# A Mixer's output stage in another order of queues, and the adaLN products moved back by three steps

## The chip, the core and the metric

The kernel runs on one NeuronCore of one Trainium2 chip. The core has five engines, each with its own instruction queue that runs strictly in order: TensorE (PE in the profile; its weight loads are PEld), VectorE (DVE), ScalarE (ACT), GpSimd (POOL) and SyncE (SP), which here only issues DMAs. PE writes its results into PSUM, eight banks of 128 x 512 f32, and the others read them there. The metric is the device time of one execution in microseconds, given as the median of several runs; lower is better.

## The reference

One layer of a streaming encoder on 1024 tokens of width 1024, f32. Three residual sub-layers, each conditioned on a vector `c`:

```python
def sandwich(x, fn, g_pre, g_post, shift, scale, gate, res_w):
    h = modulate(rmsnorm(x, g_pre), shift, scale)
    y = rmsnorm(fn(h), g_post)
    return x + res_w * gate[:, None, :] * y

mod = (silu(c) @ w_ada + b_ada).reshape(b, 3, 3, D_MODEL)        # shift, scale, gate of each sub-layer
x = sandwich(x, swiglu_1, ..., mod[:, 0, 0], mod[:, 0, 1], mod[:, 0, 2], 0.5)
x = sandwich(x, mixer,    ..., mod[:, 1, 0], mod[:, 1, 1], mod[:, 1, 2], 1.0)
x = sandwich(x, swiglu_2, ..., mod[:, 2, 0], mod[:, 2, 1], mod[:, 2, 2], 0.5)

def mixer(h, ...):                       # q k v xr yr g_att g_rec = split(h @ w_in)
    att = chunked_attention(q, k, v, rel_bias) @ w_att_o
    rec = (rg_lru(conv(xr)) * gelu(yr)) @ w_rec_o
    return (sigmoid(g_att) * att + sigmoid(g_rec) * rec) @ w_out
```

The change concerns two places: the product with `w_out` with the residual and the norm behind it, up to the first matmuls of `swiglu_2`; and the part of `mod` that belongs to the Mixer's gate and to the second SwiGLU, which is computed beside the product with `w_rec_o`.

## The kernel before

Every f32 operand of a matmul is split into a high part (rounded to the matmul's f32r format, by a copy on ACT) and a low part (the difference, by a subtraction on DVE); a product is then three matmuls, high x high, high x low, low x high (`split`, L147; `mm3`, L488). Matmuls are 128 x 128 by 128 x 512.

**Order of work.** A planner places instructions on the engines by the order of the program text and its own times. Inside `manual_schedule` the order of the text itself is the order on the engines named: in `out_phase` and in the SwiGLUs on PE, DVE, ACT and POOL. The planner always orders SP, and in `rec_out_phase` it orders all engines. A buffer belongs to a tag with a fixed count: a new tile waits until an old one of its tag has been read for the last time. Tag `u` of the scratch pool has three buffers, `raw` (weights as loaded) three, `junk` two. PSUM tag `ps` has six banks, `tr` two. Two engines that touch the same PSUM bank are put one behind the other.

**`rec_out_phase` (L1250).** For each of eight blocks n: the gate product of block n + 1 (48 matmuls), four steps of a background queue, the product with `w_rec_o` of block n (48 matmuls), the merge on DVE and its store, then four more steps of the background queue, each with a step of `out_weights`. After block 7 attention begins (first matmuls L1327).

**The background queue** holds generators (`bg`, L324; one step runs one to its next `yield`). Here they are two column sets, `ada_cols(6)` and `ada_cols(7)`, and two gates, `ada_gate(1)` and `ada_gate(2)`. Each first sums eight blocks of `w_ada`, scaled by `c` (`ada_acc`, L194): a load of 512 KB into `raw` and a DVE operation (L206, L208) per step, into `acc` of tag `u`. `ada_cols` (L214) then makes eight one-column products on PE (L222) and adds the bias on DVE. `ada_gate` (L294) takes two halves: split `acc` (tag `junk`), two matmuls with a matrix of ones (L310, L311) that spread the row over all partitions, add the bias row `bb` (tag `u`, loaded) at L312; at last the scale and a store.

**`out_phase` (L1654).** The 1024 tokens are eight row blocks `sb`, the 1024 columns two halves H1 and H2. The product is by Strassen-Winograd, seven block products (numbers 1, 2, 6, 5, 3, 7, 4), each 48 matmuls, that go into four PSUM banks `chain` (two of tag `ps`, two of tag `tr`) or four private ones. Row blocks 0 to 3 are finished after product 3, the second half of columns of blocks 4 to 7 after product 7, their first half after product 4, which is run for one row block at a time (12 matmuls each). A finished row block goes through these steps:

- `square` (L1676, ACT) of each half with its sum; `gated` (L1683, DVE) multiplies by the gate; `rate` (L1687) makes the reciprocal root, on POOL (L1690);
- `update` (L1693): `epi.update` (L414) adds to the residual row block on DVE (L418) and stores it; `epi.square` (L423) squares the new row block for the next norm on ACT (L342), the root on POOL (L343, L344);
- `epi.norm` (L429) scales the row block by that root, on DVE (L435).

When four row blocks have their norm, `epi.drain` (L439) turns the blocks of columns k = 0 to 7 into the next sub-layer's transposed input: four transposes on PE (L379) into one bank, the high part by an activation on ACT (L361), the value in f32 on ACT (L368) or DVE (L370), the low part on DVE (L354). `on_act` says which engine makes the f32 value for even and odd k.

**`head` (L759)** of the second SwiGLU: for its first two blocks of features, eight steps k of six matmuls each on the first 512 tokens (`part`, L596), with a yield behind each step at which `out_phase` puts its own last work; then the same on the other 512 tokens. Step k needs column block k.

Of the kernel before, what the change touches and what calls it, by code (L numbers as in the profile page):

```python
# [27 lines left out]
SB = S // P  # L28
# [7 lines left out]
HEAD_WAIT = 13  # L36
# [2 lines left out]
SHARE = (3, 4, 4, 5, 5)  # L39
LEFT = 40.0  # L40
GATES = (2, 0, 2, 4)
NORM_ACT = ()
DIRECT = {0: 4, 2: 3}
KEPT_FROM = 5

# [4 lines left out]
def kernel(  # L50
# [160 lines left out]
        yield None  # L211
        yield acc

    def ada_cols(v):  # L214
        acc = None
        for acc in ada_acc(v, tu):
            if acc is None:
                yield
        yield BANK
        pc = trbank("pc")  # L220
        for k in range(KB):
            nc.tensor.matmul(  # L222
                pc[:, k : k + 1], acc[:, k * P : (k + 1) * P], ones[:, 0:1], start=True, stop=True
            )
        sub, kind = divmod(v, 3)
        badd = colsA[:, 8 + v * 8 : 16 + v * 8]
        if kind == 0:
            nc.vector.tensor_tensor(scol[sub], pc[:, 0:KB], badd, op=ALU.add)
        else:
            sc = small("adat", KB)  # L230
            nc.vector.tensor_tensor(sc, pc[:, 0:KB], badd, op=ALU.add)
            nc.vector.scalar_tensor_tensor(
                acol[sub], sc, 1.0, colsA[:, 80 + sub * 8 : 88 + sub * 8], op0=ALU.add, op1=ALU.mult
            )
        yield
# [55 lines left out]
        gtile[sub] = tmp[0].tile([P, D], F32, tag="gate", bufs=1, name=nm("gate"))  # L291
        nc.sync.dma_start(gtile[sub], gate_d[sub])

    def ada_gate(sub, res_w, alloc=tu):  # L294
        v = sub * 3 + 2
        acc = None
        for acc in ada_acc(v, alloc):
            if acc is None:
                yield
        g = tmp[0].tile([P, D], F32, tag="gate", bufs=1, name=nm("gate"))  # L300
        gtile[sub] = g
        bb = tu("bb")
        nc.sync.dma_start(bb, brow(b_ada[0, v * D : (v + 1) * D]))
        for h in range(2):
            sl = slice(h * 512, (h + 1) * 512)
            ah, al = (tmp[0].tile([P, 512], F32R, tag="junk", bufs=2, name=nm("acch")) for _ in range(2))
            split(acc[:, sl], ah, al)
            yield BANK
            pg = trbank("pg")
            nc.tensor.matmul(pg, ones_r, ah, start=True, stop=False)  # L310
            nc.tensor.matmul(pg, ones_r, al, start=False, stop=True)  # L311
            nc.vector.tensor_tensor(g[:, sl], pg, bb[:, sl], op=ALU.add)  # L312
        bb2 = tu("bb2")
        nc.sync.dma_start(bb2, brow(norm_post[0, sub]))
        nc.vector.scalar_tensor_tensor(g, g, res_w, bb2, op0=ALU.mult, op1=ALU.mult)
        if sub in gate_d:
            nc.sync.dma_start(gate_d[sub], g)
        yield
# [63 lines left out]
    class Epilogue:  # L382
# [43 lines left out]
                self.todo.remove(sb)  # L426
                self.r2[sb] = rstd_of(self.xr[sb], EPS)

        def norm(self, sb):  # L429
            if sb not in self.r2:  # L430
                return
            if sb in NORM_ACT:
                nc.scalar.activation(self.y[sb], self.xr[sb], AF.Copy, scale=self.r2.pop(sb))
            else:
                nc.vector.tensor_scalar(self.y[sb], self.xr[sb], self.r2.pop(sb), None, op0=ALU.mult)  # L435
# [1218 lines left out]
    def out_phase(ops, xin, xout, make, start_h, ahead):  # L1654
# [56 lines left out]
        with tc.manual_schedule(engines=CORE_ENGINES):  # L1711
# [42 lines left out]
                rate(i)  # L1754
            for sb in range(3):
                update(sb)
            for j in product(7, chain, False):
                epi.fetch(half + j, t4)
            for i in range(half):
                add(half + i, H2, chain[i])  # L1760
                square(half + i, H2)
                if i == 0:
                    update(3)
                else:
                    epi.norm(i - 1)
            gated(4, H2)
            epi.norm(3)
            start_h()
            for n in range(half):
                sb = half + n  # L1770
                for _ in range(OUT_PAIRS):
                    if n == 0:
                        ops.load(len(ops.order))
                    mm(chain[n], n, 4, _, False, _ == OUT_PAIRS - 1)
                square(sb, H1, chain[n])
                gated(sb, H1, chain[n])
                rate(sb)
                if n < 3:
                    gated(sb + 1, H2)
                if n > 0:  # L1780
                    update(sb - 1)
                if n == 2:
                    epi.drain(2, on_act=(1, 1))
                if n == 3:
                    epi.norm(4)
                    epi.drain(1, on_act=(1, 1))
            tr_home[0] = "tr"
            for i, _ in enumerate(ahead.head()):
                if i == 1:
                    update(SB - 1)  # L1790
                if i >= HEAD_WAIT or (epi.ready and epi.ready[0][0] == 0):
                    epi.drain(1)
                if i < 3:
                    epi.norm(half + 1 + i)
            epi.drain(KB)


# [229 lines left out]
    with tc.tile_pool(name="psA", bufs=1, space=PSUM) as psA, tc.tile_pool(name="tmpA", bufs=1) as tmpA:  # L2027
# [13 lines left out]
        rec_h, rec_l, wts = lru_run.rest()  # L2041
        part = dpool.tile([D, S], F32, name="part")
        tg_dram = dpool.tile([D, S], F32, name="tg_dram")
        bgq.extend([ada_cols(6), ada_cols(7), ada_gate(1, 1.0), ada_gate(2, 0.5)])
        rec_out_phase(hh, hl, rec_h, rec_l, wts, part, out_weights())
    n_ga = sum(GATES)
    att_h, att_l = att_phase(hh, hl, wts, tg_dram, n_ga)
# [56 lines left out]
```

## Time and profile before

| | us |
|---|---|
| median of 3 runs (lowest to highest) | 2187.97 (2186.08 to 2188.87) |
| the profiled execution | 2192.95 |
| its span, from the first to the last instruction | 2191.0 |
| PE busy / DVE busy / ACT busy / POOL busy | 2143.4 / 1333.0 / 1022.9 / 666.6 |
| mean granted PE clock over the span | 0.992 |

How to read it: busy times are shares of one span on engines that run side by side, so they don't add up. A row of the timeline or of a group names the line, the engine, the operation, the tiles written and read with their shape, and in square brackets how long the engine stood idle just before and what released it. A matmul's own length is modelled; what one costs in a row of many is the distance between starts. The granted clock is 1.00 at full speed.

### The profile page before, as it was taken

What the parts mean: (1) busy time and instruction counts of PE and PEld (TensorE: products, weight loads), DVE (VectorE), ACT (ScalarE), POOL (GpSimd) and SP (SyncE); (2) the same over time, 40 slices, a digit from 0 to 9 for tenths busy, and PEclk for the clock granted to TensorE, in tenths of its full rate; (3) what the DMA queues carried; (4) which work ended last, traced back from release to release, by engine and by line L of the source; (5) the groups of instructions that cost most, each with busy time, mean ns of one, the idle gap of its engine ahead of it and who ended that gap; (6) DMA issues with size and microseconds to landing.
All of it is one profiled execution on the core that took longest, in us unless ns stands there. A gap on an engine that the chain in (4) does not pass through costs nothing.

```text
span 2191.0 us, 26876 instructions
## 1 busy us (share of the span) xinstructions
PE 2143.4 (98%) x9925; PEld 1778.1 (81%) x9925; DVE 1333.0 (61%) x1798; ACT 1022.9 (47%) x1617; POOL 666.6 (30%) x498
## 2 busy tenths in 40 slices
PE   7999999999999999999999999999999999999998
PEld 5888788888878888888798988887788888888877
DVE  7766665566457777765336666576586564544466
ACT  4433333334447777622247777435443333334443
POOL 1168885431104011000021120002068883522102
PEclk9999999999999999999999999999999999999999
DMA  9356774368575111398712013467157663347365
GB/s 325 103 188 240 248 251 156 124 241 308 179 254 181 43 41 51 115 316 290 271 40 70 26 52 102 161 211 259 56 185 261 242 215 120 107 154 275 127 231 185
DMA packets 266364, 383.55 MB, mean 175 GB/s; under 512 B 17488, under 2 KB 171256, under 8 KB 266232
## 3 DMA queue, kind: packets, MB, share of 16 engines
q1 hardware_dynamic: 253312, 335.60, 46.2%
q10 hardware_dynamic: 12920, 46.23, 5.5%
q8 instruction: 78, 1.28, 0.2%
q14 instruction: 54, 0.44, 0.1%
HBM read 275.86 MB, written 109.05 MB: 176 GB/s over the span
## 4 chain that ended last, share of the span: by engine, by line
PE 80%; DVE 7%; ACT 6%; DMA 4%; issue 2%; POOL 1%; SPq 0%; POOLq 0%; DVEq 0%; ACTq 0%
PE px L973 8%; PE pv L973 8%; PE pj L491 6%; PE pj L492 6%; PE pj L493 6%; PE psX L713 6%; PE psX L715 6%; PE psX L714 6%; PE pj L1327 5%; PE psZ L713 3%; PE psZ L715 3%; PE psZ L714 3%; PE px L1664 2%; PE pv L1374 2%; PE pv L1664 1%
## 5 line engine op out<-in xcount | busy, mean ns | idle before, releaser
L148 ACT CAST dh<-rawd 128x1024 fp32r<-128x1024 f32 x154 | 161.2, 1053 | 204.3 <-PE px L973 62.1
L149 DVE TENSOR_TENSOR dh<-rawd,dh 128x1024 fp32r<-128x1024 f32 x130 | 162.8, 1256 | 151.6 <-ACT dh L148 144.3
L704 DVE TENSOR_TENSOR wm<-raw,wm 128x512 fp32r<-128x512 f32 x152 | 158.5, 1046 | 152.0 <-ACT wm L703 147.4
L491 PE MATMUL pj<-hh,wh 128*128 128x512 f32 x562 | 223.6, 398 | 3.0 <-ACT hh L361 3.0
L492 PE MATMUL pj<-hl,wh 128*128 128x512 f32 x562 | 221.2, 394 | 1.8 <-DVE hl L354 1.8
L493 PE MATMUL pj<-hh,wl 128*128 128x512 f32 x562 | 221.0, 393 | 0.0
L973 PE MATMUL px<-dh,dh 128*128 128x512 f32 x608 | 187.5, 389 | 0.2 <-DVE dh L149 0.2
L973 PE MATMUL pv<-dh,dh 128*128 128x512 f32 x528 | 163.4, 390 | 2.9 <-DVE dh L149 2.7
L149 POOL TENSOR_TENSOR wl<-raw,wh 128x1024 fp32r<-128x1024 f32 x20 | 48.3, 2422 | 322.5 <-ACT wh L148 278.0
L911 POOL TENSOR_TENSOR act<-act,act 128x512 f32<-128x512 f32 x54 | 86.1, 1594 | 169.0 <-DMA act<-act 119.4
L973 PE MATMUL px<-dh 128*128 128x512 f32 x352 | 137.3, 390 | 0.0
L973 PEld LDWEIGHTS px<-dh,dh 128*128 128x128 f32 x608 | 114.0, 188 | 24.7 <-DVE dh L149 1.1
L491 PEld LDWEIGHTS pj<-hh,wh 128*128 128x128 f32 x562 | 106.8, 190 | 24.7 <-ACT hh L361 3.2
L492 PEld LDWEIGHTS pj<-hl,wh 128*128 128x128 f32 x562 | 106.9, 190 | 24.5 <-DVE hl L354 2.7
L493 PEld LDWEIGHTS pj<-hh,wl 128*128 128x128 f32 x562 | 106.9, 190 | 22.5
L973 PEld LDWEIGHTS pv<-dh,dh 128*128 128x128 f32 x528 | 98.6, 188 | 25.5 <-DVE dh L149 5.2
L713 PE MATMUL psX<-hh,wm 128*128 128x512 f32 x296 | 115.4, 390 | 1.4 <-ACT mixes L736 1.2
L713 PE MATMUL psX<-hs,wm 128*128 128x512 f32 x296 | 115.5, 390 | 0.1
L715 PE MATMUL psX<-hs,wm 128*128 128x512 f32 x296 | 115.2, 389 | 0.0
L714 PE MATMUL psX<-hl,wm 128*128 128x512 f32 x296 | 115.2, 389 | 0.0
L714 PE MATMUL psX<-hs,wm 128*128 128x512 f32 x296 | 115.2, 389 | 0.0
L715 PE MATMUL psX<-hh,wm 128*128 128x512 f32 x296 | 115.2, 389 | 0.0
(344 smaller groups left out, 5498.3 us busy)
## 6 DMA issues: line engine op xcount, KB each, us to landing
rawa<-in_w_ada_dram SPq DMA_DIRECT2D x56, 512.0 KB, 5.1
rawd<-acts SPq DMA_DIRECT2D x88, 256.0 KB, 3.9
rawd<-downs SPq DMA_DIRECT2D x88, 256.0 KB, 3.6
raw<-in_w_in_dram SPq DMA_DIRECT2D x44, 512.0 KB, 3.9
raw<-in_ffn_w_gu_dram SPq DMA_DIRECT2D x43, 512.0 KB, 4.8
sr<-in_ffn_w_gu_dram SPq DMA_DIRECT2D x39, 512.0 KB, 5.8
act<-act SPq DMA_DIRECT2D x37, 512.0 KB, 5.0
acts<-act ACTq DMA_DIRECT2D x36, 512.0 KB, 4.1
```

The lines of the kernel that those rows point to most:

```text
L148: nc.scalar.copy(hi, raw)
L149: (eng or nc.vector).tensor_tensor(lo, raw, hi.bitcast(F32), op=ALU.subtract)
L491: nc.tensor.matmul(dst, wh[:, kk, :], xhk[:, sl], start=first, stop=False)
L492: nc.tensor.matmul(dst, wh[:, kk, :], xlk[:, sl], start=False, stop=False)
L493: nc.tensor.matmul(dst, wl[:, kk, :], xhk[:, sl], start=False, stop=last)
L704: nc.vector.tensor_tensor(t[:, 1], src, t[:, 0].bitcast(F32), op=ALU.subtract)
L713: nc.tensor.matmul(dst, t[:, 0, kk, :], xh, start=first and kk == 0, stop=False, skip_group_check=True)
L714: nc.tensor.matmul(dst, t[:, 0, kk, :], xl, start=False, stop=False, skip_group_check=True)
L715: nc.tensor.matmul(dst, t[:, 1, kk, :], xh, start=False, stop=last and kk == 3, skip_group_check=True)
L911: nc.gpsimd.tensor_tensor(o, p, q, op=op)
L973: nc.tensor.matmul(dst, a_[:, 0, tk], w_[:, 1, :], start=first and n == 0, stop=last and n == 2, skip_group_check=True,)
L1327: nc.tensor.matmul(d, a[:, k, :], b[k][:, sl], start=k == 0 and i == 0, stop=k == KB - 1 and i == 2)
```

## The change

In `rec_out_phase` each column set of the background queue waits three steps more between its last accumulation and its products, each half of a gate two steps more between split and products.

In `out_phase`, from the end of product 3 on: the norms of row blocks 0 and 2 run on ACT, as an activation with a scale, those of 1 and 3 on DVE (before, all four on DVE). The steps of row blocks 4 to 7 are put into another order among the transposes of column blocks 0 to 7: column block 0 is transposed before the third part of product 4, blocks 1 and 2 before the fourth, blocks 3 to 7 behind the first five steps of `head`. The squares of the finished row blocks 4 to 7 (`epi.square`) stand behind activations of transposed blocks in ACT's queue; before, `update` issued them together with the update. The last row block's gating and rate run behind the first step of `head`. Which f32 values are made on ACT changes: column blocks 0, 2, 3, 4 and 6 (before 0, 1, 2, 4 and 6).

```diff
-NORM_ACT = ()
...
-    def ada_cols(v):
+    def ada_cols(v, later=0):
         acc = None
         for acc in ada_acc(v, tu):
             if acc is None:
                 yield
+        for _ in range(later):
+            yield
         yield BANK
...
-    def ada_gate(sub, res_w, alloc=tu):
+    def ada_gate(sub, res_w, alloc=tu, later=0):
...
             split(acc[:, sl], ah, al)
+            for _ in range(later):
+                yield
             yield BANK
...
-        def norm(self, sb):
+        def norm(self, sb, on_act=False):
             if sb not in self.r2:
                 return
-            if sb in NORM_ACT:
+            if on_act:
                 nc.scalar.activation(self.y[sb], self.xr[sb], AF.Copy, scale=self.r2.pop(sb))
...
             for sb in range(3):
                 update(sb)
+            epi.norm(0, True)
             for j in product(7, chain, False):
                 epi.fetch(half + j, t4)
             for i in range(half):
                 add(half + i, H2, chain[i])
+                if i == 2:
+                    epi.norm(2, True)
                 square(half + i, H2)
                 if i == 0:
                     update(3)
-                else:
-                    epi.norm(i - 1)
+                if i == 1:
+                    epi.norm(1)
+            epi.norm(3)
             gated(4, H2)
-            epi.norm(3)
             start_h()
-            for n in range(half):
-                sb = half + n
-                for _ in range(OUT_PAIRS):
-                    if n == 0:
-                        ops.load(len(ops.order))
-                    mm(chain[n], n, 4, _, False, _ == OUT_PAIRS - 1)
-                square(sb, H1, chain[n])
-                gated(sb, H1, chain[n])
-                rate(sb)
-                if n < 3:
-                    gated(sb + 1, H2)
-                if n > 0:
-                    update(sb - 1)
-                if n == 2:
-                    epi.drain(2, on_act=(1, 1))
-                if n == 3:
-                    epi.norm(4)
-                    epi.drain(1, on_act=(1, 1))
+
+            def last(n):
+                for j in range(OUT_PAIRS):
+                    mm(chain[n], n, 4, j, False, j == OUT_PAIRS - 1)
+                square(half + n, H1, chain[n])
+
+            def close(sb):
+                gated(sb, H1, chain[sb - half])
                 rate(sb)
+
+            ops.load(len(ops.order))
+            last(0)
+            close(4)
+            gated(5, H2)
+            last(1)
+            epi.update(4)
+            close(5)
+            epi.drain(1, on_act=(1, 1))
+            last(2)
+            epi.square(4)
+            gated(6, H2)
+            epi.update(5)
+            close(6)
+            epi.drain(2)
+            epi.norm(4)
+            last(3)
             tr_home[0] = "tr"
             for i, _ in enumerate(ahead.head()):
+                if i >= HEAD_WAIT or (epi.ready and epi.ready[0][0] == 0):
+                    epi.drain(1, on_act=(1, 0) if i > 0 else (1, 1))
+                if i == 0:
+                    epi.square(5)
+                    gated(7, H2)
+                    close(7)
                 if i == 1:
-                    update(SB - 1)
-                if i >= HEAD_WAIT or (epi.ready and epi.ready[0][0] == 0):
-                    epi.drain(1)
-                if i < 3:
-                    epi.norm(half + 1 + i)
+                    epi.update(6)
+                if i == 2:
+                    epi.square(6)
+                    epi.update(7)
+                if i == 3:
+                    epi.square(7)
+                    epi.norm(5)
+                if i == 5:
+                    epi.norm(6)
+                if i == 6:
+                    epi.norm(7)
             epi.drain(KB)
...
-        bgq.extend([ada_cols(6), ada_cols(7), ada_gate(1, 1.0), ada_gate(2, 0.5)])
+        bgq.extend([ada_cols(6, 3), ada_cols(7, 3), ada_gate(1, 1.0, later=2), ada_gate(2, 0.5, later=2)])
```

## The prediction

> **What bounds the kernel now.** The page first: the span and the engines' shares.
>
> ```profile
> span 2191.0 us, 26876 instructions
> PE 2143.4 (98%) x9925; PEld 1778.1 (81%) x9925; DVE 1333.0 (61%) x1798; ACT 1022.9 (47%) x1617; POOL 666.6 (30%) x498
> ```
>
> TensorE (PE) is busy 98% of the span, and the change removes no matmul. It can win only idle time of PE and time at a low clock. The windows of 50 us show where these lie in the two stages that the change touches (columns: window, its length, then busy us of PE, PEld, DVE, ACT, POOL, granted clock, DMA share, GB/s):
>
> ```profile
> 1000.00:1050.00 50.00, 46.92 (x205) 38.07 (x204) 28.72 (x35) 11.96 (x18) 0.00 (x0) 0.98 0.87 290
> 1500.00:1550.00 50.00, 42.54 (x184) 33.74 (x183) 35.34 (x55) 27.91 (x55) 15.55 (x24) 0.93 0.54 191
> 1600.00:1650.00 50.00, 49.87 (x221) 40.96 (x220) 38.97 (x42) 21.21 (x39) 39.84 (x26) 1.00 0.58 205
> ```
>
> The first window lies in `rec_out_phase` (890 to 1085) with the modulation products beside it; the second holds the end of `out_phase` and the start of the second SwiGLU's `head`; the third is the least filled of the windows from 1550 to 2100, so what is won before carries to the end. PE's waits there (total, times, longest), first 890 to 1110, then 1480 to 1580:
>
> ```profile
> PE pg L311 <- DVE acch L149: 1.6, 1, 1.6
> PE pg L310 <- ACT acch L148: 1.5, 1, 1.5
> PE pc L222 <- DVE acc L208: 1.3, 1, 1.3
> PE pj L1327 <- ACT wh L148: 0.9, 1, 0.9
> ```
>
> ```profile
> PE pj L491 <- ACT hh L361: 3.0, 1, 3.0
> PE pt L379 <- ACT h L368: 2.7, 1, 2.7
> PE pj L492 <- DVE hl L354: 1.8, 2, 0.9
> ```
>
> So 4.4 us stand before small products of the modulation and 7.5 us before the first matmuls and transposes of `head`. Each stall costs more than its idle time, because the clock falls after it. PE's timeline, and three windows laid around the stalls:
>
> ```profile
> 936.54 0.39 PE L493 MATMUL pj<-hh,wl 128*128 128x512 f32 x1
> 938.22 2.81 PE L222 MATMUL pc<-ones_r,acc 128*128 128x1 f32 x16 [1.29 <-DVE acc L208]
> 940.89 0.77 PE L491 MATMUL pj<-rh,wh 128*128 128x512 f32 x1
> 946.05 0.40 PE L491 MATMUL pj<-rh,wh 128*128 128x512 f32 x1
> 976.01 1.84 PE L222 MATMUL pc<-ones_r,acc 128*128 128x1 f32 x16
> 1501.48 19.52 PE L1664 MATMUL px<-wu,mo 128*128 128x512 f32 x84
> 1550.01 0.39 PE L491 MATMUL pj<-hh,wh 128*128 128x512 f32 x1
> 1558.52 0.48 PE L491 MATMUL pj<-hh,wh 128*128 128x512 f32 x1
> 1560.35 0.48 PE L491 MATMUL pj<-hh,wh 128*128 128x512 f32 x1
> ```
>
> ```profile
> 936.00:946.05 10.05, 8.76 (x34) 7.16 (x33) 4.95 (x6) 3.08 (x4) 0.00 (x0) 0.66 0.98 311
> 1045.00:1055.20 10.20, 7.12 (x19) 4.99 (x19) 5.48 (x7) 3.66 (x4) 0.00 (x0) 0.67 1.00 335
> 1524.00:1550.00 26.00, 18.54 (x75) 14.12 (x74) 15.55 (x23) 14.68 (x23) 5.11 (x8) 0.87 0.36 122
> ```
>
> A matmul of 512 columns costs PE 19.52/84 = 0.23 us; six of them with a block's four transposes take 1560.35 - 1558.52 = 1.83, so the transposes 0.45. **Stall a** (938): idle 938.22 - 936.54 - 0.23 = 1.45; the sixteen column products take 2.81 against 1.84 later on, +0.97; the twelve matmuls from 940.89 to 946.05 take 5.16 against 2.76, +2.4. Together 4.8 us. **Stall b** (1045 to 1055): 19 matmuls in 10.2 us, worth 4.4: 5.8 us lost. **Stall c** (head): 26 us at clock 0.87 lose 3.4 us beside the 7.5 idle.
>
> **The change part by part: `out_phase`.** Why PE waits at the head is read on ACT and DVE:
>
> ```profile
> 1511.30 0.63 ACT L1680 ACTIVATE junk<-y 128x512 bf16<-128x512 f32 x1 [1.50 <-DVE y L1674]
> 1521.75 1.06 ACT L342 ACTIVATE junk<-xr 128x1024 bf16<-128x1024 f32 x1 [2.68 <-DVE xr L418]
> 1526.16 1.06 ACT L342 ACTIVATE junk<-xr 128x1024 bf16<-128x1024 f32 x1 [2.68 <-DVE xr L418]
> 1527.21 0.76 ACT L361 ACTIVATE hh<-pt,scol,acol 128x512 fp32r<-128x512 f32 x1
> 1524.79 1.28 DVE L418 SCALAR_TENSOR_TENSOR xr<-y,sq,xr 128x1024 f32<-128x1024 f32 x1
> ```
>
> Block 0's activation (1527.21) is queued on ACT behind the square of row block 5 (1526.16), which waits 2.68 us for its update on DVE (1524.79). That is the in-order queue which the change turns round: activations first, squares behind them. The unit costs:
>
> ```profile
> L361 ACT ACTIVATE hh<-pt,scol,acol 128x512 fp32r<-128x512 f32 x8 | 6.1, 768 | 1.6 <-PE pt L379 1.5
> L435 DVE TENSOR_SCALAR y<-xr,rstd 128x1024 f32<-128x1024 f32 x8 | 6.0, 746 | 0.0
> L354 DVE TENSOR_TENSOR hl<-h,hh 128x512 fp32r<-128x512 f32 x8 | 5.5, 691 | 7.9 <-ACT h L368 7.8
> L1685 DVE TENSOR_TENSOR y<-px,gate 128x512 f32<-128x512 f32 x4 | 2.7, 687 | 2.2 <-ACT junk L1680 2.2
> L370 DVE TENSOR_SCALAR h<-pt,acol,scol 128x512 f32<-128x512 f32 x3 | 2.4, 810 | 0.4 <-ACT hh L361 0.4
> L1828 ACT ACTIVATE x<-x,rstd x4: 1132/1148/1151, 10.2 to 61.2; 128x1024 f32<-128x1024 f32 x4
> ```
>
> No instruction is added. Norms 0 and 2 go from DVE (0.75 each) to ACT (1.15 each, by the same form at start-up, L1828). Norm 0 falls into ACT's idle 1.50 us before 1511.30, so it is free; norm 2 pushes ACT's next squares back by about 1 us, and the first `gated(4, H1)` behind them by 0.2 us by my layout. The Trainium skill, "ScalarE: Activation LUTs", section "Rules for kernel authors", says that multiplications belong on VectorE; the rows agree on the price (1.15 against 0.75), and by the rule the sum would be 0.8 us worse if both stood on the path.
>
> I lay the new order out by hand. Product 7 (48 matmuls) ends at 1501.48 + 11.0 = 1512.5. `last(0)`, `last(1)` end at 1518.0. The transposes of block 0 follow (0.5): its norms are done by 1516, norm 3 being the last. `last(2)` ends at 1521.2, the transposes of 1 and 2 at 1522.2, `last(3)` at 1525.0. ACT writes block 0 between 1518.7 and 1520.1, behind square (5, H1); DVE writes its low part behind `update(4)` and `gated(5, H1)`, about 1521.9. The first six matmuls of `head` start at 1525.0 with 3 us in hand: the waits of 3.0 and 0.9 us go. What is late next: block 4's transposes need a PSUM bank, either that of block 3 (free about 1528.1) or that of the fourth chain (free after `gated(7, H1)`, about 1530.0), against a PE that comes for it at 1527.9; and blocks 6 and 7, whose activations stand behind squares 6 and 7, which wait for updates of 1.28 us on DVE. From `gated(4, H1)` at 1517.5 to block 7's low part DVE has 7 gatings, 4 updates, 8 low parts, 3 activations and 2 norms: 7 x 0.69 + 4 x 1.28 + 8 x 0.69 + 3 x 0.81 + 2 x 0.75 = 19.4 us, or 1536.9 without a wait; I find 2 to 3 us of waits in it. Block 7's six matmuls then end at 1540.1 with the one bank, 1541.3 with the other. Before, they end at 1550.01. PE's own work would end at 1525.0 + 8 x 1.38 + 5 x 0.45 = 1538.3. So the head wins 8.7 to 9.9 us, at most 12. The 2 to 3 us left idle are in small pieces; if they fall together, the clock falls again at up to 1.7 us. The stores of x2 move with their updates on SP; behind them stand the weights of the third SwiGLU block, used only after the 32 steps of `head`. I take **8.9**. Should the order not bind as I read it, the bound on the other side is stall c staying as it is, 0.
>
> The Trainium skill, "TensorE: Matmul & The Clock Gate", Part 1, has the clock halved only after at least one idle window of about 3.4 us. Here 1.45 us idle with sixteen one-column products brought 0.66 over 10 us, so the rows are stricter. By the rule no remainder here costs clock, and the sum would be nearer 9.9.
>
> **The part in `rec_out_phase`.** The background queue takes 8 steps per block, 64 in all. A column product stood two steps behind its last accumulation and now stands five behind; a gate's products one behind their split, now three. Column set 6: accumulated at step 9, multiplied at 11 before, both ahead of block 1's 48 matmuls; now at 14, behind them. That is 11 us of cover where 1.45 lacked: **stall a goes, 4.8 us**. Set 7: 23 and 28 with 48 matmuls between; no wait before, none after. Its cost if the cover fails is that of stall a.
>
> Gates: the rows behind stall b, and of what follows it:
>
> ```profile
> 1010.50 0.39 PE L310 MATMUL pg<-acch,ones_r 128*128 128x512 f32 x1
> 1045.33 1.04 ACT L148 CAST wh<-raw 128x1024 fp32r<-128x1024 f32 x1 [2.96 <-DMA raw<-in_w_rec_o_dram]
> 1022.36 0.75 DVE L206 TENSOR_SCALAR acc<-rawa,c_act 128x1024 f32<-128x1024 f32 x1
> 1040.44 1.28 DVE L208 SCALAR_TENSOR_TENSOR acc<-rawa,c_act,acc 128x1024 f32<-128x1024 f32 x1 [0.40 <-DMA rawa<-in_w_ada_dram]
> 1055.19 1.29 DVE L312 TENSOR_TENSOR gate<-pg,bb 128x512 f32<-128x512 f32 x2 [0.68 <-DMA bb<-in_b_ada_dram]
> ```
>
> The second half's cast stood on ACT behind a weight cast that waited 2.96 us for its DMA. In the new order the second half of either gate is split and multiplied within one group of four steps (41 and 44, 57 and 60), so no matmul is put between by the text; only the planner can. Gate 1's halves now stand where no modulation load runs (its last is step 36, the next gate's first 45), so its weights come in time. Gate 2's loads move from steps 35 to 42 to 45 to 52, and no matmul is left between its sum and its product. Its first accumulation came 11.9 us after gate 1's first product (1010.50 to 1022.36), when gate 1's scratch was free; its eight took 19.4 (to 1041.72), the split 1.3: 32.6 us after gate 1's product, against three times 48 matmuls, 33.1 us. It is just ready when block 6's matmuls end. So stall b may vanish (5.8), come back, or come twice (-5.8). I take about half, **3**. Loads per gate stay eight of 512 KB; SP passes them in the same order relative to each other, later relative to the weights.
>
> **Sum.** 8.9 + 4.8 + 3 = 16.7; less 0.2 for norm 2: 16.5 us. The profiled execution took 2192.95 (span 2191.0 and 1.95 around it), 5 us above the median of 2187.97; the gain is a difference inside the span and I carry it over: **2171.5**.
>
> **The rivals.**
>
> *Everything goes* (0.15): 9.9 + 4.8 + 5.8 = 20.5, 2167.5. For: PE's bound in the head is 12. Against: gate 2's tight end.
>
> *The gates' stalls come back twice* (0.20): 8.9 + 4.8 - 5.8 = 7.9, 2180. For: nothing lies between split and product of the second halves. Against: fewer loads compete.
>
> *The head stays bound by ACT and DVE* (0.10): the later bank (1.2) and two low-clock windows (3.4) leave 9.9 - 4.6 = 5.3, with 7.8 from the Mixer 13: 2175. ScalarE's dearer norms belong here.
>
> *The waits only change place* (0.08): no stall is shorter in sum, 2188 within 4.4 us.
>
> *Slower* (0.05): gate 2's sum spills past `rec_out_phase`. Attention's first product (L1327, 0.9 us of wait now) takes PSUM banks that L312 must have read, and block 7 covers only 11 + 1.3 us after block 6. Behind the sum come two splits, two products, the bias row and L312, about 6 us; so the sum must end within 6 us of block 6, and each us later costs one. To be slower by 4.4 us against a gain of 16.5 it must end 27 us after block 6, its 19.4 us beginning 7 us after it: only if the three-buffer scratch tag stays taken, where I find its start 20 us before block 6 ends. Price from there: 2193 and more.
>
> **How the numbers follow.** My forecast has 0.42. The range takes in the first four, from 2166 to 2184. Faster by over 0.2% (4.4 us; about what a measurement can tell): 0.42 + 0.15 + 0.20 + 0.10 = 0.87; same 0.08; slower 0.05.
>
> **What would show it.** Right: no wait of PE at L222; the first L491 of `head` without idle time ahead; block 7's matmuls done 8 to 10 us earlier counted from product 7's end; ACT's squares 4 to 7 behind activations. Wrong: an idle of 2 us or more before L379, a clock under 0.9 in that window, waits of PE at L310 or L311 as long as before, or a wait over 2 us at the first L1327. If attention's waits change, the planner has moved what I hold fixed.

## The result and the profile after

| | before | after |
|---|---|---|
| median, us (lowest to highest, runs) | 2187.02 (2184.78 to 2188.87, 4) | 2174.28 (2171.58 to 2176.83, 4) |
| ratio of the times, 95% interval | 1 | 0.9942 (0.9925 to 0.9959) |
| profiled execution: span, us | 2191.0 | 2169.7 |

The change makes the kernel 12.7 us faster (9.0 to 16.4 by the interval). The two profiled spans differ by more, 21.3 us: the profiled execution of before (2192.95) took longer than any of its timed runs, that of after is the fastest of its four. Lines from about L300 on now have numbers 3 higher (L491 is L494, L379 is L382, L418 is L421, L342 is L345). The page of after:

```profile
span 2169.7 us, 26880 instructions
PE 2130.5 (98%) x9925; PEld 1767.7 (81%) x9925; DVE 1335.1 (62%) x1796; ACT 1025.5 (47%) x1619; POOL 665.3 (31%) x498
```

PE has the same 9925 matmuls and is busy 12.9 us less. A matmul at a low clock is busy longer (0.63 us instead of 0.39 in the rows behind stall a), so this part of the gain is clock; the other 8.4 us of the 21.3 are idle time. The windows of after, in the columns used before:

```profile
1000.00:1050.00 50.00, 50.00 (x222) 41.19 (x221) 31.70 (x41) 16.43 (x26) 0.00 (x0) 1.00 0.92 316
1500.00:1550.00 50.00, 48.78 (x243) 39.23 (x242) 33.04 (x51) 30.94 (x53) 7.82 (x14) 1.00 0.36 122
```

In the second window 243 matmuls and transposes ran where 184 did before, at a clock of 1.00 where it was 0.93. (It is the same stretch of time, not quite the same work: after is about 12 us further on there.) PE's waits in after, first 890 to 1110, then 1480 to 1580:

```profile
PE pj L1330 <- DVE tg L1269: 2.0, 1, 2.0
PE pg L314 <- DVE acch L148: 1.5, 1, 1.5
```

```profile
PE pj L495 <- DVE hl L357: 1.1, 1, 1.1
```

Of the 7.5 us of waits at `head`, 1.1 are left. At the small products one wait of three is left (L314), and the wait at attention's first product (L1330, in before L1327) has grown from 0.9 to 2.0. PE's timeline:

```profile
945.09 1.84 PE L223 MATMUL pc<-ones_r,acc 128*128 128x1 f32 x16
...
1489.29 16.68 PE L1667 MATMUL px<-wu,mo 128*128 128x512 f32 x72
1512.66 0.39 PE L494 MATMUL pj<-hh,wh 128*128 128x512 f32 x1
1516.16 0.66 PE L382 MATMUL pt<-ident,y 128*128 128x128 f32 x4
1526.53 0.50 PE L495 MATMUL pj<-hl,wh 128*128 128x512 f32 x1 [1.08 <-DVE hl L357]
1527.79 0.39 PE L494 MATMUL pj<-hh,wh 128*128 128x512 f32 x1
```

Column set 6 is now multiplied at 945.09 without a wait and takes 1.84 us, its price at full clock. Product 7 starts at 1489.29; 48 matmuls of 16.68/72 us put its end at 1500.4. The matmul at 1527.79 is the first behind block 7's six: 27.4 us after product 7's end, where before it was 1550.01 - 1512.5 = 37.5. The head is 10.1 us shorter. Why is read on ACT:

```profile
1506.65 0.77 ACT L364 ACTIVATE hh<-pt,scol,acol 128x512 fp32r<-128x512 f32 x1
...
1509.86 1.05 ACT L345 ACTIVATE junk<-xr 128x1024 bf16<-128x1024 f32 x1
...
1520.50 1.06 ACT L345 ACTIVATE junk<-xr 128x1024 bf16<-128x1024 f32 x1 [0.94 <-DVE xr L421]
1521.56 0.76 ACT L364 ACTIVATE hh<-pt,scol,acol 128x512 fp32r<-128x512 f32 x1
1522.22 0.77 ACT L371 ACTIVATE h<-pt,scol,acol 128x512 f32<-128x512 f32 x1
1523.08 1.06 ACT L345 ACTIVATE junk<-xr 128x1024 bf16<-128x1024 f32 x1
1524.14 0.76 ACT L364 ACTIVATE hh<-pt,scol,acol 128x512 fp32r<-128x512 f32 x1
```

Block 0's activation (1506.65) stands ahead of the first square of row blocks 4 to 7 (1509.86), where before it stood behind two of them and behind their waits of 2.68 us. The one square that still waits, 0.94 us at 1520.50, does so when PE has blocks in hand: no wait of PE follows until block 7. The last square (1523.08) stands ahead of block 7's activation (1524.14), and that is the 1.1 us that are left. At the end of `rec_out_phase` DVE shows where the new wait comes from:

```profile
1059.11 1.23 DVE L148 TENSOR_TENSOR wl<-raw,wh 128x1024 fp32r<-128x1024 f32 x1 [1.62 <-ACT wh L147]
1060.25 1.28 DVE L1269 SCALAR_TENSOR_TENSOR tg<-tg,pj 128x512 f32<-128x512 f32 x2
1061.45 0.68 DVE L148 TENSOR_TENSOR acch<-acc,acch 128x512 fp32r<-128x512 f32 x1
1068.94 1.29 DVE L315 TENSOR_TENSOR gate<-pg,bb 128x512 f32<-128x512 f32 x2 [6.81 <-DMA bb<-in_b_ada_dram]
1071.94 1.23 DVE L318 SCALAR_TENSOR_TENSOR gate<-gate,bb 128x1024 f32<-128x1024 f32 x1 [1.71 <-DMA bb<-in_norm_post_dram]
1073.08 1.27 DVE L1269 SCALAR_TENSOR_TENSOR tg<-tg,pj 128x512 f32<-128x512 f32 x2
```

Gate 2 is now so late that its two bias rows are loaded while block 7 runs. DVE stands 6.81 us and 1.71 us for them, and the last merge of block 7 (L1269, 1073.08), which attention's first product waits for, is queued behind. The first three rows belong to the wait at L314: the low part of gate 2's second half (1061.45) stands behind a weight's subtraction, which waited 1.62 us for its cast, and behind block 6's merge.

### The profile page after: what moved, and what is told of

Read it like the earlier page. It is cut to its first block, busy times and chain, and to the rows that moved or that the text cites. A ratio compares the mean times of both kernels' runs of the same rounds, so it can differ in the third digit from the quotient of the medians.

```text
span 2169.7 us, 26880 instructions
## 1 busy us (share of the span) xinstructions
PE 2130.5 (98%) x9925; PEld 1767.7 (81%) x9925; DVE 1335.1 (62%) x1796; ACT 1025.5 (47%) x1619; POOL 665.3 (31%) x498
## 4 chain that ended last, share of the span: by engine, by line
PE 82%; DVE 6%; DMA 6%; ACT 4%; issue 1%; SPq 1%; POOL 0%; POOLq 0%; DVEq 0%; ACTq 0%
PE px L976 8%; PE pv L976 7%; PE pj L494 7%; PE pj L495 7%; PE pj L496 7%; PE psX L716 6%; PE psX L718 6%; PE psX L717 6%; PE pj L1330 6%; PE psZ L716 3%; PE psZ L718 3%; PE psZ L717 3%; PE px L1667 2%; DMA rawd<-downs 2%; PE pv L1377 2%; PE pv L1667 2%
## 5 line engine op out<-in xcount | busy, mean ns | idle before, releaser
L494 PE MATMUL pj<-hh,wh 128*128 128x512 f32 x562 | 221.1, 394 | 0.0
L494 PEld LDWEIGHTS pj<-hh,wh 128*128 128x128 f32 x562 | 105.5, 188 | 21.5 <-DVE a L529 0.3
```

The costliest lines, as they stand in the source:

```text
L494: nc.tensor.matmul(dst, wh[:, kk, :], xhk[:, sl], start=first, stop=False)
```

## The experiments

Each kernel was timed beside the kernel before on the same chip. "Stages" are distances between first matmuls in a profile: `rec_out_phase` from the last gate product of the recurrence to attention's first product, attention from there to the first merge matmul, the output stage from the first matmul with `w_out` to the second SwiGLU's first matmul with mixed weights (`psX<-hh,wm`), which is behind all of `head`.

| kernel | median, us (runs) | before, us | ratio (95%) | rec_out | attention | output stage |
|---|---|---|---|---|---|---|
| before | | | | 192.0 | 316.8 | 161.2 |
| before_again | 2188.61 (1) | | | 188.4 | 316.8 | 161.2 |
| after | 2174.28 (4) | 2187.02 | 0.9942 (0.9925, 0.9959) | 184.0 | 316.8 | 151.2 |
| after_again | 2175.15 (6) | 2187.95 | 0.9936 (0.9921, 0.9950) | 183.7 | 316.9 | 151.3 |
| mixer_only | 2178.29 (5) | 2187.95 | 0.9950 (0.9936, 0.9964) | 189.6 | 316.9 | 151.5 |
| later_only | 2186.39 (12) | 2187.95 | 0.9987 (0.9978, 0.9997) | 185.5 | 318.4 | 161.5 |
| squares_first | 2183.63 (10) | 2186.70 | 0.9981 (0.9972, 0.9991) | 186.0 | 318.3 | 159.6 |
| norms_dve | 2174.07 (4) | 2186.70 | 0.9934 (0.9915, 0.9952) | 185.5 | 318.4 | 152.9 |
| cols_only | 2177.84 (4) | 2186.70 | 0.9952 (0.9934, 0.9970) | 185.8 | 316.8 | 152.6 |
| gates_only | 2177.38 (4) | 2186.70 | 0.9949 (0.9932, 0.9967) | 186.9 | 316.8 | 152.0 |
| after_third | 2175.31 (5) | 2187.87 | 0.9941 (0.9929, 0.9953) | 183.8 | 316.9 | 152.3 |
| spread | 2178.09 (5) | 2187.87 | 0.9956 (0.9942, 0.9970) | 182.4 | 318.7 | 151.4 |
| spread_sq7 | 2175.51 (5) | 2187.87 | 0.9944 (0.9931, 0.9956) | 184.9 | 319.2 | 150.3 |
| square7_later | 2173.68 (5) | 2187.87 | 0.9936 (0.9924, 0.9949) | 184.4 | 318.5 | 150.0 |

The theory was that of the prediction, called A below: two separate gains, one from ACT's order in the head and one from matmuls put between the modulation's sums and their products. The rivals differ from run to run and stand in the expectations.

**The two parts by themselves.** mixer_only is the changed kernel with the old distances of the small products; later_only is the kernel before with the new ones.

```diff
mixer_only, against after:
-        bgq.extend([ada_cols(6, 3), ada_cols(7, 3), ada_gate(1, 1.0, later=2), ada_gate(2, 0.5, later=2)])
+        bgq.extend([ada_cols(6), ada_cols(7), ada_gate(1, 1.0), ada_gate(2, 0.5)])
later_only, against before:
-        bgq.extend([ada_cols(6), ada_cols(7), ada_gate(1, 1.0), ada_gate(2, 0.5)])
+        bgq.extend([ada_cols(6, 3), ada_cols(7, 3), ada_gate(1, 1.0, later=2), ada_gate(2, 0.5, later=2)])
```

> The new order in out_phase alone; the background queue as before. Theory A (two independent gains, each with its own stalls): 9 to 10.5 us faster than before (ratio about 0.9955), PE's waits at the head of the second SwiGLU down from 7.5 us to 1.1, the column products and gate products in rec_out_phase waiting as before (4.4 us in all, within a us or two, since they hang on DMA times). Theory B (the gain of the medians comes from the Mixer's background products, and the head's gain is given back later, as FFN2's loads come no earlier): within 3 us of before.

> The later steps of the background queue alone; out_phase as before. Theory A: faster by what is left of 12.7 us, 2 to 5 us (ratio about 0.998 to 0.999), less than the 8.1 us that the two profiles differ by in rec_out_phase, because the profile of before caught longer stalls there than its usual run has; no wait at the column products, one of about 1.5 us at the second half of the last gate, and the head's waits of 7.5 us unchanged. Theory B: 8 us or more faster.

> The changed kernel once more, for its spread and a second profile. Theory A: 12 to 14 us faster than before; its profile shows again one wait at the last gate (1 to 2 us), one at attention's first product (about 2 us), one at the head (1.1 us), and the stages start within 1 us of each other as counted from their own beginnings. If the waits in rec_out_phase differ between the two profiles by some us, DMA times set them anew in each execution.

> The kernel before once more, one look, for a second profile. Theory A (its first profile was a long execution, 5 us above the median): the head's waits are the same 7.5 us to 0.2, and the stalls at the column products and the gates are shorter than 4.8 and 5.8 us by 2 to 6 us in all. Rival: the same stalls to 0.3 us, and the 5 us lie elsewhere (start, attention, the end).

By the ratios mixer_only gains 10.9 us (7.9 to 14.0) and later_only 2.8 (0.7 to 4.8); together 13.7, and the changed kernel beside them 14.0. Within these intervals the two parts add. The output stage is 10 us shorter in mixer_only and unchanged in later_only, so the whole gain of the first part lies there. `rec_out_phase` is shorter by the second part alone. before_again tells something on the prediction's source: its `rec_out_phase` took 188.4 us where the profile of before has 192.0. PE's waits there (890 to 1110):

```profile
PE pc L222 <- DVE acc L208: 1.8, 1, 1.8
PE pg L311 <- DVE acch L149: 1.6, 1, 1.6
PE pj L1327 <- ACT wh L148: 0.9, 1, 0.9
```

The wait at L310 that the prediction priced within stall b isn't there. In both profiles the gate's cast on ACT is queued behind a weight cast that waits for its load, for 2.96 us in before and 1.87 in before_again. The same kernel has other stalls in another execution, so one profile of this stage is one draw. In the head before_again has waits of 6.3 us where before has 7.5, and the stage is as long, 161.2.

**The squares ahead again.** squares_first is the changed kernel with one thing undone: the square of each finished row block 4 to 7 stands again directly behind its update.

```diff
             last(1)
-            epi.update(4)
+            update(4)
...
-            epi.square(4)
...
-            epi.update(5)
+            update(5)
...
-                    epi.square(5)
...
-                    epi.update(6)
+                    update(6)
...
-                    epi.square(6)
-                    epi.update(7)
+                    update(7)
...
-                    epi.square(7)
```

> The changed kernel with one thing undone: the squares of finished row blocks 4 to 7 stand right behind their updates again, ahead of the activations of transposed blocks; transposes, norms and the background queue as changed. If the order of squares and activations on ACT is the cause of the head's gain (theory A): the square of block 5 waits for its update until about 1 us after block 1's activation could start, the activations of blocks 1, 2, 5 and 6 come 2 to 4 us late, PE waits 3 to 6 us in the head again and the stage from the first product with w_out to the second SwiGLU's first mixed product is 154 to 158 us long, against 151.2 (changed) and 161.2 (before). If the earlier transposes alone are the cause (rival): 151 to 152 us.

The output stage grows to 159.6, of which 1.2 us are a wait for a load of `w_out` that after doesn't have: 158.4 against 151.2, so 7 of the 10 us go back. That is more than the 154 to 158 expected. The idle time came as forecast, 4.8 us of waits on ACT and DVE in the head against 1.1 in after; the rest is clock, 0.93 from 1500 to 1550 against 1.00, or 3.5 us, which the expectation had left out. PE's waits in squares_first, 1480 to 1580, and then ACT's timeline:

```profile
PE pj L495 <- DVE hl L357: 1.8, 2, 0.9
PE pj L494 <- ACT hh L364: 1.7, 1, 1.7
...
PE pt L382 <- DVE h L373: 1.0, 1, 1.0
PE pt L382 <- ACT h L371: 0.3, 1, 0.3
```

```profile
1517.87 1.06 ACT L345 ACTIVATE junk<-xr 128x1024 bf16<-128x1024 f32 x1 [2.04 <-DVE xr L421]
...
1518.93 1.43 ACT L364 ACTIVATE hh<-pt,scol,acol 128x512 fp32r<-128x512 f32 x2
...
1531.77 1.06 ACT L345 ACTIVATE junk<-xr 128x1024 bf16<-128x1024 f32 x1 [2.86 <-DVE xr L421]
...
1532.83 0.76 ACT L364 ACTIVATE hh<-pt,scol,acol 128x512 fp32r<-128x512 f32 x1
```

It is the picture of before: ACT stands 2.04 and 2.86 us for an update on DVE, with an activation that PE needs queued behind it. The same work on the same engines, in the other order, costs 7 us by the stage. By the medians it costs more, 9.6 us against norms_dve beside it, so 7 of 10 is one profile's share. What is left of the head's gain, 3 us by the stages, would belong to the rest of the new order (the earlier transposes, norms and gatings); no run takes these apart.

**The norms back on DVE.** norms_dve is the changed kernel with norms 0 and 2 on DVE.

```diff
-            epi.norm(0, True)
+            epi.norm(0)
...
-                    epi.norm(2, True)
+                    epi.norm(2)
```

> The changed kernel with all four norms of row blocks 0 to 3 on DVE again. Theory A: the norms' engine is worth less than 1 us here, since ACT has idle time for one and PE comes for the transposes after both; the stage stays within 0.8 us of 151.2, the first gating of block 4's last product within 0.4 us of where it was. Rival (the ScalarE rule): 0.8 us or more shorter, because ACT's 2.3 us for two norms stand on the path; other rival (DVE was the bound): 1.5 us or more longer.

No difference can be measured: 0.9934 (0.9915 to 0.9952) against the changed kernel's 0.9941, 0.9936 and 0.9942, and an output stage of 152.9, less a wait of 1.6 us for a load of `w_out`, so 151.3. The norms' 1.14 us on ACT (at 1497.52 and 1501.98 in after) lie under product 7 and the first part of product 4, and so do the 0.75 us on DVE. Whether the first gating of product 4 stays in its place can't be read, because the wait for `w_out` falls just ahead of it.

**Each kind of small product alone.** cols_only keeps the later column products, gates_only the later gate products; the head is the new one in both.

```diff
cols_only:
+        bgq.extend([ada_cols(6, 3), ada_cols(7, 3), ada_gate(1, 1.0), ada_gate(2, 0.5)])
gates_only:
+        bgq.extend([ada_cols(6), ada_cols(7), ada_gate(1, 1.0, later=2), ada_gate(2, 0.5, later=2)])
```

> The changed kernel with later steps for the column sets alone, the gates one step behind their split. Theory A (a wait goes where 48 matmuls come to stand between sum and product): no wait at the column products; the gates now begin at steps 29 and 43, so that the sum and the products of gate 1 (37 and 39) and of gate 2 (51 and 53, with block 6 between) lie otherwise than before: a wait of 1 to 4 us at gate 1 and about 1.5 us at a second half; rec_out_phase 185 to 189 us long, against 183.8 (changed) and 190.0 (mean of three without later steps). Rival (the column sets are the whole gain): 184.

> The changed kernel with later steps for the gates alone. Theory A: the wait at the first column products stays (1.3 to 2.3 us, with the low clock behind it 4 to 6 us); the gates begin at steps 23 and 39, so that 48 matmuls stand between the two halves' products (35 and 38, 51 and 54), and no gate product waits; attention's first product waits about 0.9 us as before; rec_out_phase 184.5 to 187 us. Rival (it is only the number of steps that counts, not what stands between): a wait of 1 to 1.6 us at a second half, as in the changed kernel, 188 or more.

PE's waits from 890 to 1110 in cols_only:

```profile
PE pg L313 <- ACT acch L147: 3.0, 1, 3.0
PE pj L1330 <- DVE tg L1269: 0.8, 1, 0.8
```

and in gates_only:

```profile
PE pj L1330 <- DVE tg L1269: 2.8, 1, 2.8
PE pc L223 <- DVE acc L207: 2.3, 1, 2.3
```

Each edit removes its own wait and leaves the other's. The 3.0 us of cols_only stand at gate 2's second half (1055.18); gate 1, where 1 to 4 us were expected, doesn't wait. (Gate 2 begins at step 41, not 43: its first product stands 33.7 us, three times 48 matmuls, behind gate 1's.) In gates_only no gate product waits at all, though the distances are those of after: each column set takes three steps less, and with that the halves' products fall behind 48 matmuls. In after the second half of either gate is split and multiplied within one group of four steps. The planner puts the same few matmuls between at both. Gate 2's then waits 1.5 us; gate 1's doesn't, because DVE makes its low part at once (1026.20; the cast ends at 1025.98). In all seven kernels with the queue of after gate 1's second half waits 0 to 0.35 us, gate 2's 1.1 to 2.3. So the number of steps between doesn't decide. A group's end, with its 48 matmuls, covered every gate product in gates_only; without one it depends on what else ACT and DVE have queued. The wait at attention's first product is 0.8 us in cols_only and 2.8 in gates_only, where 0.9 was expected: it comes with the gates' delay, not with the columns'.

**Distances chosen by counting, and the last square.** spread puts every gate product four steps behind its split, so that a group's end lies between, and column set 7 last; square7_later moves the last square behind block 7's activation; spread_sq7 has both.

```diff
spread:
-        bgq.extend([ada_cols(6, 3), ada_cols(7, 3), ada_gate(1, 1.0, later=2), ada_gate(2, 0.5, later=2)])
+        bgq.extend([ada_cols(6, 2), ada_gate(1, 1.0, later=3), ada_gate(2, 0.5, later=3), ada_cols(7, 1)])
square7_later:
-                if i == 3:
+                if i == 4:
                     epi.square(7)
                     epi.norm(5)
```

> The changed kernel with the background queue in the order column set 6, gate 1, gate 2, column set 7, and the distances chosen by counting steps: a product with the matrix of ones always stands four steps behind its split, so that 48 matmuls lie between the two for either half of either gate; column set 7's products come last, behind block 7's 48 matmuls. Theory A (a product waits only where no 48 matmuls lie between it and the work it needs; what is late at the end of rec_out_phase is the bias row of gate 2, whose loads stand in DVE's queue ahead of the first pass at attention): no wait of PE at the gates' products or the column products (1.1 to 1.6 us in the changed kernel), the first product of attention waits 0.9 us again instead of 2.0, so rec_out_phase 181 to 182.5 us instead of 183.7 to 184.0, and the time 1 to 2.5 us under the changed kernel of the same call. Rival (the stalls are set by the traffic of the modulation loads, so they turn up at another place when these move): a new wait of 1 to 3 us at some load or product, rec_out_phase 184 to 187, no gain. The head unchanged at 151.2 us.

> The order of the kernel spread, and beside it the square of row block 7 and the norm of row block 5 one step of head later, behind the activation of column block 5. Theory A: both savings add: rec_out_phase 181 to 182.5 us, from the first w_out matmul to the second SwiGLU 150 to 150.3 us instead of 151.2, the time 2 to 3.5 us under the changed kernel. Rival (the transposes of column block 6 then wait for the later norms): the stage stays at 151.2 or grows to 152.

> The changed kernel with only the square of row block 7 and the norm of row block 5 one step of head later. Theory A: the last wait in head (1.1 us before the low part of column block 3, whose f32 value stands on ACT or DVE behind work of row block 7) goes or shrinks to a half: the stage from the first w_out matmul to the second SwiGLU 150.1 to 150.6 us instead of 151.2; time 0 to 1 us under the changed kernel, within its measurement. Rival (the wait is that of the PSUM bank and of DVE, not of ACT): unchanged at 151.2 us, or 0.5 to 1 us longer because the second half of head needs the norms of blocks 5 to 7 in time.

> The changed kernel once more, on the same chip as the three beside it. All theories: rec_out_phase 183.5 to 186 us, the stage of w_out up to the second SwiGLU 151.2 us, time 2172 to 2177 us and 10 to 15 us under the kernel before.

The expectation of square7_later names column block 3; the wait is block 7's. Its mechanism held: that kernel has no wait in the head at all and an output stage of 150.0, 1.2 us less than after. ACT's timeline there:

```profile
1528.17 0.77 ACT L371 ACTIVATE h<-pt,scol,acol 128x512 f32<-128x512 f32 x1
1528.84 0.77 ACT L364 ACTIVATE hh<-pt,scol,acol 128x512 fp32r<-128x512 f32 x1
1529.50 1.05 ACT L345 ACTIVATE junk<-xr 128x1024 bf16<-128x1024 f32 x1
```

The median is 1.6 us under after_third, which the intervals don't tell apart; only the stage length shows the gain.

spread met its theory halfway. No gate product waits, in either kernel with this order. But the modulation loads now run to the end of the phase, and column set 7's last sum is late: it ends at 1071.13 in spread, after all of block 7's 48 matmuls, so here a group's end was no cover. spread, 890 to 1110, and then spread_sq7:

```profile
PE pc L223 <- DVE acc L207: 1.6, 1, 1.6
PE pj L1330 <- DVE adat L232: 0.8, 1, 0.8
```

```profile
PE pc L223 <- DVE acc L207: 2.9, 1, 2.9
PE pj L1330 <- DVE adat L232: 1.3, 1, 1.3
```

`rec_out_phase` is 182.4 and 184.9 us, the first as expected and the second not, and both times miss the expectation: they are no better than after_third's. The rival took the place: the stall turned up at another product. Over the nine profiles in which columns and gates are both later (the queue of after, or that of spread) the phase takes 182.4 to 186.0 us, and each has waits of 1 to 3 us somewhere.

## Why the prediction was right, and where its sizes were off

The forecast was 2171.5 in 2166 to 2184; the time was 2174.28. The mechanisms held, and the gain was 12.7 us where 16.5 were forecast. Two later measurements of both kernels give 12.8 and 12.6, so the difference of 4 us is hardly chance in one measurement. The number alone would not have picked the mechanism: 2174.28 is nearer to the 2175 of the rival whose head stays bound than to the forecast, and the wide range took in three rivals beside it. The stages decide.

- **The head, forecast 8.9, measured 10.** Mechanism as stated: activations first, squares behind, block 0 ready before PE comes for it. Block 4's transposes (1516.16, 15.8 us after product 7's end) came where block 3's bank was forecast to be free (1528.1 - 1512.5 = 15.6), so it was the earlier of the two banks; the other was read until 1518.0, by the gating at 1517.35. The forecast lay between the two and allowed for a remainder of 2 to 3 us of idle time: 27.6 us after product 7's end with the one bank, 28.8 with the other. It was 27.4. Late behind square 7 was block 7 alone, by 1.1 us, and the clock stayed at 1.00. By the rule of the Trainium skill ("TensorE: Matmul & The Clock Gate", Part 1) no remainder here was to cost clock, and the trace agrees at this place.
- **Stall a, forecast 4.8: gone.** 945.09 has no idle time in front and the full clock. gates_only and mixer_only, which keep the old distance, keep waits of 2.3 us there. Wait and slow matmuls together (what their steps take over the full-clock step, 0.23 us for 512 columns) took 4.7, 5.2 and 5.8 us in before, before_again and mixer_only, so the size was right.
- **Stall b, forecast 3, about half of its 5.8: 1.3.** The wait at L310 is not in after (nor, it turned out, in before_again), and that at the low part of the second half, one of the signs named for being wrong, stayed at 1.5 us. The prediction had stated that the text puts no matmul between its split and its product; in gates_only, with 48 matmuls between, it is gone. Gate 1, whose weights were forecast to come in time, didn't wait in after.
- **The step that failed: "the gain is a difference inside the span and I carry it over".** The 7.8 us for `rec_out_phase` came from an execution whose stall b was long. Counted in the same way, waits and slow matmuls at the gates took 6.2 us there, but 2.2 in before_again and 2.8 in mixer_only, which have the same queue. The stage took 192.0 us against 188.4 and 189.6, a mean of 190.0. The seven profiles with the queue of after (after, after_again, after_third, later_only, squares_first, norms_dve, square7_later) take 183.7 to 186.0, in the mean 184.7, and their gates still cost 1.5 to 3.4 us, in the mean 2.4 against 3.7. The gain is 5.3, not 7.8: 5.2 at column set 6 and 1.3 at the gates, less 1.3 for the wait of the next point. The profiled execution was 5 us over the median; of the 4.3 by which it exceeds before_again, 3.6 lie in this stage. A gain that consists of removing such stalls cannot be carried over whole.
- **The wait at attention's first product, not in the sum.** It grew from 0.9 to between 1.6 and 2.8 us in the kernels with the queue of after. Over 2 us was a sign named for being wrong: after has 1.95, five of the other six exceed it. The prediction had it only as the slower rival's place, from which "the sum must end within 6 us of block 6". The sum was in time; DVE's queue was not, as its rows showed: the bias rows' loads stand ahead of the last merge. Loading these rows earlier wasn't tried.
- **A low clock at the start of attention, not in the sum.** Attention takes 316.8 us in the three profiles without the later products, and in the others either 316.8 (5 of 11) or 318.3 to 319.2 (6 of 11). The mean over the eleven is 1.0 us longer; the last section shows where it lies. The prediction's price for one low-clock window, 1.7 us, is near the 1.5 to 2.4 that each of the six lost, but it stood with the head, where none came.

Head 10.0, `rec_out_phase` 5.3, attention -1.0: 14.3 from stage lengths of single profiles, against 12.7 by the medians, whose interval reaches from 9.0 to 16.4. What is left is 1.6 us. About 0.5 of it is the choice of profile: over the seven profiles with the head just as in after, the output stage takes 151.7 us in the mean, not 151.2, because a wait of 0.2 to 1.3 us for a load of `w_out` stands in four of them. The rest isn't located.

Of the rivals, "everything goes" needed both gates free, and one wasn't. "The gates' stalls come back twice" and "the head stays bound" didn't come. "The waits only change place" holds for nothing in the head, but for most of the waiting in `rec_out_phase`: with attention's first product PE's waits there sum to 5.0 us in the mean of the three profiles without later products and still to 4.0 in the seven with the queue of after. So 1.0 of the 5.3 us is idle time; 4.3 us are the same matmuls at a higher clock (0.96 to 0.98 over the phase in the three, 1.00 in the seven), 3.4 of them at and behind column set 6. The slower rival came in small: its place, at a price of 1 to 2 us. ScalarE's dearer norms decided nothing, as norms_dve shows; the advice of the Trainium skill ("ScalarE: Activation LUTs", "Rules for kernel authors") to put multiplications on VectorE is neither borne out nor refuted by it, since both engines had the time.

## What to carry to other kernels

On an in-order engine, put an operation that must wait for another engine (here a square behind an update) after those whose inputs lie ready and that the bound engine is waiting for; the total of work need not change, and here the order alone was worth 7 us of 2188 by the length of its stage. To cover a small product's latency, count what the schedule really puts between its input and it, not the steps: three steps within one group left gate 2's second half waiting, while one step over a group's end gives up to 11 us, and no more when the input itself is late, as in spread. Look at the clock as well as at the waits: a stage can get faster though its waits mostly move. Price a stall that a DMA sets from several executions, and before delaying work look at what else on its engine's queue is delayed with it.

## What the runs showed of the hardware

A wait of PE of some 2 us costs clock in one execution and none in the next. after and norms_dve stand before the same wait at attention's first product. Two windows laid at its end (in the columns used above), first after:

```profile
1072.71:1074.41 1.70, 0.00 (x0) 0.00 (x1) 1.65 (x3) 0.60 (x1) 1.02 (x1) 1.00 0.25 99
1074.41:1077.81 3.40, 3.40 (x15) 2.83 (x16) 0.00 (x0) 0.00 (x0) 1.36 (x1) 1.00 0.89 311
```

and norms_dve:

```profile
1074.75:1076.45 1.70, 0.00 (x0) 0.00 (x1) 1.65 (x3) 0.49 (x1) 1.13 (x1) 1.00 0.24 99
1076.45:1079.85 3.40, 3.40 (x8) 2.73 (x9) 0.00 (x0) 0.00 (x0) 1.23 (x1) 0.51 0.91 306
```

PE was idle for 1.95 us in the one and 2.06 in the other. In after it goes on at full clock with 15 matmuls in the next 3.4 us; in norms_dve the clock is 0.51 and 8 matmuls run. That is the 1.6 us by which attention differs. The length of the wait doesn't decide: in gates_only PE stood idle longer, and its next matmul follows at full clock.

```profile
1079.87 0.47 PE L1330 MATMUL pj<-hh,wh 128*128 128x512 f32 x1 [2.79 <-DVE tg L1269]
1080.18 0.40 PE L1330 MATMUL pj<-hl,wh 128*128 128x512 f32 x1
```

after_again waited 2.10 us without loss, square7_later 2.10 with it. In spread 0.76 us of wait were enough, behind sixteen one-column products that had themselves waited 1.59. In all six profiles with a longer attention the slow matmuls stand within its first 4.3 us, 0.43 us from start to start, over a stretch of 3.1 to 4.3 us. The Trainium skill, "TensorE: Matmul & The Clock Gate", Part 1, says that activity is counted in windows of about 3.4 us that run freely, whatever the kernel does: the length of the slow stretch and its coming and going fit that. That a whole window must be idle does not fit as it stands, since 2.06 us of idle time were enough.
